# Three seven-product chunk pairs in each wide down panel, and two of their weight sums added by DMA

## The chip, the cores and the metric

The kernel runs on one core of a Trainium2 chip. The metric is the device time of one execution in microseconds, as the median of several runs. A profile of one execution comes with it: busy times, waits and DMA transfers by engine and by line of the kernel.

The engines are TensorE (PE in the profile; its weight loads are PEld), VectorE (DVE), ScalarE (ACT), GpSimd (POOL) and SyncE (SP). SP and GpSimd start DMA transfers here; a queue starts its transfers in the order in which they stand, and one that has to wait holds up those behind it.

## The reference

A decoder trunk of two layers works on 256 tokens of width 2048 in float32. The first layer mixes tokens by gated linear attention, the second by forgetting attention, and each also attends to 256 memory tokens. What the change touches is the gated MLP with hidden width 5632 that ends each layer:

```python
def conv_ffn(h, w_up, conv_w, conv_b, w_down):
    u = causal_dwconv(h @ w_up, conv_w, conv_b)
    a, val = split_cols(u, [FFN_HIDDEN, FFN_HIDDEN])
    return (jax.nn.silu(a) * val) @ w_down
```

The result of `conv_ffn` is added to the residual stream `x`.

## The kernel before

**Products in parts.** A float32 product is made of three matmuls. Each operand is split into a high part (a copy rounded to the format that TensorE multiplies, `fp32r`) and a low part (the rest). High x high, low x high and high x low are added in one PSUM bank. For weights, ScalarE makes the high part (`whi`, an ACTIVATE) and VectorE the low part (`wlo`, a subtraction) from the loaded tile `raw`. These tiles are 128 x 1024 and each of the three names has four buffers.

**The MLP.** The hidden width is 44 chunks of 128, taken in three parts of 16, 16 and 12 chunks (`PARTS`). For each part the kernel computes the up-projections, convolves and gates them (`convolve`), and keeps the activations in parts as tiles `m` (`A`, `B` or `mix` in the profile). Then it multiplies the part by `w_down`. In the first two parts of each layer, output columns 0 to 1023 are done in two ordinary panels of 512 columns, and columns 1024 to 2047 in one wide panel, `pair_tm` (line 338), which takes one chunk of 128 hidden channels after another. There are thus four such panels in the kernel, two a layer.

**A plain chunk and a seven-product pair.** For a plain chunk `pair_tm` loads 128 x 1024 weights and makes four products (two halves of the tokens by two halves of the columns), 12 matmuls (line 377), each over 512 columns. Two chunks together are a 2 x 2 block product. For the pairs that begin at a chunk in `SEVEN` (0 and 4) the kernel uses the Winograd form of Strassen's method: seven products, 21 matmuls (the helper `mm`, line 363), in place of eight products and 24. It needs four sums of activation blocks and four sums of weight blocks.

The activation sums are made in `convolve`, in temporary tiles `tsum` and then split into `asum`, one such tile for each pair. The weight sums stand in `pair_tm`: `ta` holds two of them and `tb` two (both `tsum` in the profile), 128 x 512 each, added by VectorE from the loaded weights at lines 393 to 396:

```python
V.tensor_tensor(ta[:, :512], b12, b11, ALU.subtract)
V.tensor_tensor(ta[:, 512:], b22, b12, ALU.subtract)
V.tensor_tensor(tb[:, :512], b22, ta[:, :512], ALU.subtract)
V.tensor_tensor(tb[:, 512:], b21, tb[:, :512], ALU.subtract)
```

After that `split_more` (lines 325 and 326) casts and splits `ta` and `tb` like other weights. In order, a pair's products are `p1` (with `b11`), `p2` and `p3` (with the second chunk's weights), `p5` and `p7` (with `ta`), `p6` and `p4` (with `tb`). The products `p1`, `p5`, `p6` and `p7` stay in four PSUM banks until the last pair of the panel; then one copy and seven additions (lines 406 to 409, and `add_to`, line 435) combine them and add them to `x`. The plain chunks add to other banks, which are read at the panel's end.

**Buffers.** The function `room` gives out the temporary tiles. In layer 0, `tsum` tiles share two buffers (tag `blk`), `ev` (the combination's temporary) has tiles of its own, and each pair's `asum` has one. In layer 1, `tsum` tiles share three buffers (tag `wlo` of the pool `op`), and `asum` and `ev` share three others (tag `whi`).

**Order.** The kernel is written as one long sequence, and a planner orders it at build time: it simulates a timeline and gives each engine, as it comes free, the ready instruction of the highest priority. `high_priority(offset=AHEAD)` moves loads, splits and weight sums some 300 places ahead. On the chip each engine and each DMA queue keeps that order, and waits on semaphores for its data and its buffers. All weight loads are on SP's queue, and `wp` is an array in which the host has laid out the weights in the order of use. For the chunks in `SEVEN` the host stores the two column halves of a chunk in reverse (`cols[::-1]`), so that `b12` comes first.

Of the kernel before, what the change touches and what calls it, by code (L numbers as in the profile page):

```python
# [13 lines left out]
F32 = mybir.dt.float32  # L14
# [3 lines left out]
ALU = mybir.AluOpType  # L18
PSUM = bass.MemoryType.PSUM

P = 128
# [17 lines left out]
NUNIT = 1024  # L39
AHEAD = 300  # L40
WARM = 9

SEVEN = (0, 4)

FV_PARTS = ((0, 376), (376, 764), (764, 1152), (1152, 1536))

# [9 lines left out]
def _panels():  # L56

    full = list(range(KC))  # L60
    out = []

    def fm(key, w, c0, kcs=full):
        out.append((key, w, kcs, [(c0, 256)], 4))

    def tm(key, w, c0, n, kcs=full, more=()):
        out.append((key, w, kcs, [(c0, n), *more], 2))

    tm(("mv", 0), ("mem_w_kv", 0), 512, 512)
    for l in range(2):  # L70
        tm(("mk", l), ("mem_w_kv", l), 0, 512)
    tm(("mv", 1), ("mem_w_kv", 1), 512, 512)
    tm(("gv", 0), ("gla_w_in", 0), G_V, DV, more=[(G_R, RANK)])
    tm(("mq", 0), ("gla_w_in", 0), G_MQ, 512)
    for h in range(GLA_H):
        tm(("gqk", h), ("gla_w_in", 0), G_Q + h * DK, DK, more=[(G_K + h * DK, DK)])
        if h == GLA_H - 1:
            tm(("og", 0), ("gla_w_in", 0), G_OG, 512)
        if h:
            tm(("gv", h), ("gla_w_in", 0), G_V + h * DV, DV)  # L80
    for j in range(1, 3):
        tm(("og", j), ("gla_w_in", 0), G_OG + j * 512, 512)
    late = list(range(12, 16)) + list(range(12))

    def ffn(l):
        for p, (lo, hi) in enumerate(PARTS):
            for j in range(lo, hi, 2):
                tm(("up", l, j), ("ffn_w_up", l), j * P, 2 * P, more=[(HID + j * P, 2 * P)])
            last = p == len(PARTS) - 1
            for f in range(4 if last else 2):  # L90
                tm(("down", l, p, f), ("ffn_w_down", l), f * 512, 512, list(range(lo, hi)))
            for k in range(0 if last else hi - lo):
                cols = [(1024, 512), (1536, 512)]
                out.append((("pair", l, p, k), ("ffn_w_down", l), [lo + k], cols[:: -1 if k in SEVEN else 1], 1))

    for f in range(4):
        tm(("wo", 0, f), ("gla_w_out", 0), f * 512, 512, late)
    ffn(0)
    for j in range(3):
        tm(("fk", j), ("fox_w_kv", None), F_K + j * 512, 512)  # L100
    for j, (lo, hi) in enumerate(FV_PARTS):
        more = [] if j else [(F_L, FOX_H)]
        tm(("fv", j), ("fox_w_kv", None), F_V + lo, hi - lo, more=more)
    for j in range(2):
        fm(("mq", 1, j), ("fox_w_in", 0), FOX_H * HD + j * 256)
    for j in range(6):
        fm(("fq", j), ("fox_w_in", 0), j * 256)
    for f in range(4):
        tm(("wo", 1, f), ("fox_w_out", 0), f * 512, 512, late)
    ffn(1)  # L110
    return out

# [29 lines left out]
def _trunk(ctx: ExitStack, tc: tile.TileContext, xt, xtok, memt, wp, wgu, gns, gfin, cnv, par, msk, out):  # L142
    nc = tc.nc
    where, _ = _layout()
    V, S, TE = nc.vector, nc.scalar, nc.tensor
# [192 lines left out]
    def pair_tm(units, src, sums, room, out):  # L338

        bank = {}  # L340

        def new(name, tag):
            bank[name] = pacc.tile([P, 512], F32, name="acc", tag="acc") if tag == "acc" else work(tag, 2 if tag == "s" else 1)

        for name, tag in (("p1", "acc"), ("p2", "o"), ("p3", "s"), ("p5", "acc"), ("p7", "acc"), ("p6", "acc"), ("p4", "s"),
                          ("x", "t")):
            new(name, tag)
        begun = set()
        n = len(units)
        plan = []  # L350
        k = 0
        while k < n:
            if k in SEVEN:
                plan.append(("seven", k))
                k += 2
            else:
                plan.append(("plain", k))
                k += 1
        end = [i for i, (kind, _) in enumerate(plan) if kind == "seven"][-1]

        def mm(name, x, w, last):
            for i, (a, b) in enumerate(((0, 0), (1, 0), (0, 1))):
                r = TE.matmul(bank[name], x[a], w[b], start=name not in begun, stop=last and i == 2)  # L363
                begun.add(name)
            return r

        def tok(k, b):
            return [src[k][:, part, b * P : (b + 1) * P] for part in range(2)]

        for i, (kind, k) in enumerate(plan):  # L370
            if kind == "plain":
                w = split_unit(units[k])
                last = k == n - 1
                for low in range(2):
                    for name, b, h in (("p2", 0, 0), ("p3", 0, 1), ("p4", 1, 0), ("x", 1, 1)):
                        for part in range(2 - low):
                            r = TE.matmul(bank[name], tok(k, b)[part], w[low][:, h * 512 : (h + 1) * 512],  # L377
                                          start=name not in begun, stop=last and low == 1)
                            begun.add(name)
                last_mm.append(r)  # L380
            else:
                ra, rb = load_unit(units[k]), load_unit(units[k + 1])
                b12, b11, b21, b22 = ra[:, :512], ra[:, 512:], rb[:, :512], rb[:, 512:]
                st = [[sums[k][:, part, j, :] for part in range(2)] for j in range(4)]
                done = i == end
                w = split_more(b11, 512)
                mm("p1", tok(k, 0), [t[:, :512] for t in w], done)
                w = split_more(rb, 1024)
                mm("p2", tok(k + 1, 0), [t[:, :512] for t in w], False)
                mm("p3", st[3], [t[:, 512:] for t in w], False)  # L390
                with tc.high_priority(offset=AHEAD):
                    ta, tb = room("t"), room("t")
                    V.tensor_tensor(ta[:, :512], b12, b11, ALU.subtract)
                    V.tensor_tensor(ta[:, 512:], b22, b12, ALU.subtract)
                    V.tensor_tensor(tb[:, :512], b22, ta[:, :512], ALU.subtract)
                    V.tensor_tensor(tb[:, 512:], b21, tb[:, :512], ALU.subtract)
                w = split_more(ta, 1024)
                mm("p5", st[0], [t[:, :512] for t in w], done)
                mm("p7", st[2], [t[:, 512:] for t in w], done)
                w = split_more(tb, 1024)  # L400
                mm("p6", st[1], [t[:, :512] for t in w], done)
                last_mm.append(mm("p4", tok(k + 1, 1), [t[:, 512:] for t in w], False))
                if done:
                    one, two = room("e")
                    three = room("f")
                    S.activation(one, bank["p1"], AF.Copy)
                    V.tensor_tensor(two, bank["p6"], one, ALU.add)
                    V.tensor_tensor(three, bank["p7"], two, ALU.add)
                    V.tensor_tensor(two, bank["p5"], two, ALU.add)
                    out(0, 1, two)  # L410
                    out(1, 1, three)
                    out(1, 1, bank["p5"])
                    out(1, 0, three)
                    out(0, 0, one)
        ends.append(r)
        for name, b, h in (("p2", 0, 0), ("p3", 0, 1), ("p4", 1, 0), ("x", 1, 1)):
            out(b, h, bank[name])
# [14 lines left out]

    def add_to(f):

        return lambda b, a: V.tensor_tensor(x[f][:, b, :], x[f][:, b, :], a, ALU.add)

    def turned(pool, bank, width, col, parts=False):

# [846 lines left out]
    def ffn(l, nx, h, m, ys, zs, landing, then, room, spare=None, last=None):  # L1285
        with tc.tile_pool(name=f"ffn{l}", bufs=1) as fp:
# [9 lines left out]
            sums = {}  # L1296

            def convolve(j, i, z, seven):
# [19 lines left out]
                if seven:  # L1318
                    (a11, a21), (a12, _) = [[r[:, b * P : (b + 1) * P] for b in range(2)] for r in rs]
                    a22 = rs[1][:, P:]  # L1320
                    t = room("s")[:, :512].rearrange("p (j n) -> p j n", j=4)
                    V.tensor_tensor(t[:, 0, :], a21, a22, ALU.add)
                    V.tensor_tensor(t[:, 1, :], t[:, 0, :], a11, ALU.subtract)
                    V.tensor_tensor(t[:, 2, :], a11, a21, ALU.subtract)
                    V.tensor_tensor(t[:, 3, :], a12, t[:, 1, :], ALU.subtract)
                    sums[i] = room(i)
# [19 lines left out]
            for p, (lo, hi) in enumerate(PARTS):  # L1346
# [18 lines left out]
                add_out(("down", l, p), m, hooks={(0, 2): lambda: close(1), (1, 4 if end else 3): lambda: close(0)}, **down)  # L1365
                if not end:
                    units = [where[("pair", l, p, k)][0] for k in range(hi - lo)]
                    pair_tm(units, m, sums, room, lambda b, h, a: add_to(2 + h)(b, a))

    def preparing(name, dst, pool, far, kept=None, tag="blk"):  # L1370

# [39 lines left out]
    with tc.tile_pool(name="stash", bufs=1) as st:  # L1411
# [4 lines left out]
        with tc.tile_pool(name="turn1", bufs=1) as tp:  # L1416
# [3 lines left out]
            def room(kind):  # L1420
                if kind in ("t", "s"):
                    return tp.tile([P, NUNIT], F32, name="tsum", tag="blk", bufs=2)
                if kind == "e":
                    return [tp.tile([P, 512], F32, name=f"ev{i}", tag=f"ev{i}") for i in range(2)]
                if kind == "f":
                    return tp.tile([P, 512], F32, name="ev2", tag="ev2")
                return tp.tile([P, 2, 4, P], F32R, name="asum", tag=f"asum{kind}")
# [12 lines left out]
    with tc.tile_pool(name="store", bufs=1) as op:  # L1440
# [44 lines left out]
        def room(kind):  # L1485
            if kind in ("t", "s"):
                return op.tile([P, NUNIT], F32, name="tsum", tag="wlo", bufs=3)
            if kind == "e":
                t = op.tile([P, NUNIT], F32, name="ev", tag="whi", bufs=3)
                return t[:, :512], t[:, 512:]  # L1490
            if kind == "f":
                return op.tile([P, 512], F32, name="ev2", tag="ev2")
# [74 lines left out]
```

## Time and profile before

| | |
|---|---|
| median of 3 runs | 2233.59 us (2232.02 to 2234.88) |
| the profiled execution | 2233.26 us |
| its span, first to last instruction | 2231.5 us |
| matmuls | 10405 |
| weight sums on VectorE, lines 393 to 396 | 8 each (two pairs in four panels) |
| DMA instructions of GpSimd in the profile | none listed |
| moved by DMA | 513.34 MB, mean 230 GB/s |

A line of a group or a tile names the line of the kernel, the engine, the operation, the tile written and those read (`wlo<-raw,whi`), the shape and the count (`x16`); durations are in ns as least, median and most. A line of a timeline gives start and duration in microseconds, and in brackets the time that the engine had been idle and what ended it. A line of waits gives the instruction that waited, what it waited for, the sum in microseconds, the count and the longest. A line with two times and a colon is one stretch of the execution, with each engine's busy time and its number of instructions. Matmuls overlap in the pipeline, so the time that one costs is read from start to start and not from its duration.

### The profile page before, as it was taken

To read this page: it belongs to the slowest core of one execution; us is meant where nothing else is said; L and a number is where in the kernel's file an instruction comes from. 1 tells how busy PE (TensorE), PEld (TensorE's weight loads), DVE (VectorE), ACT (ScalarE), POOL (GpSimd) and SP (SyncE) were. 2 spreads that over 40 slices of the span, in tenths; PEclk is the share of its full clock that TensorE was granted. 3 is DMA by queue.
4 is the path that set the end of the run, shared out by engine and by line. 5 is a ranking of instruction groups with operands and counts; after the bars stand their busy time and mean duration, and the time that the engine had idled before them with its cause. 6 is when DMAs were issued, how large, how long until landed. Compare 5 with 4: busy or idle time off the path is not lost.

```text
span 2231.5 us, 29658 instructions
## 1 busy us (share of the span) xinstructions
PE 2220.2 (99%) x10405; PEld 1869.1 (84%) x10405; DVE 1647.4 (74%) x2754; ACT 1200.5 (54%) x1779; POOL 3.4 (0%) x19
## 2 busy tenths in 40 slices
PE   9999999999999999999999999999999999999998
PEld 7888888888888888888888998888888888888886
DVE  7768977668777687866777569666877677775776
ACT  6655664555554455545565455454655455553554
POOL 0000000000000000000000000000000000000000
PEclk9999999999999999999999999999999999999999
DMA  9777667777776777667787767778786678766774
GB/s 348 231 222 223 194 187 244 250 234 247 246 223 205 227 241 244 204 213 237 240 244 251 214 195 244 226 244 258 242 242 201 217 237 242 242 200 217 240 245 142
DMA packets 183053, 513.34 MB, mean 230 GB/s; under 512 B 20588, under 2 KB 66296, under 8 KB 182776
## 3 DMA queue, kind: packets, MB, share of 16 engines
q1 hardware_dynamic: 182328, 510.66, 73.2%
q8 instruction: 81, 1.33, 0.2%
q10 hardware_dynamic: 576, 0.79, 0.1%
q14 instruction: 68, 0.56, 0.1%
HBM read 468.63 MB, written 42.74 MB: 229 GB/s over the span
## 4 chain that ended last, share of the span: by engine, by line
PE 98%; DMA 1%; DVE 1%; ACT 0%; SPq 0%; issue 0%; DVEq 0%
PE acc L310 71%; PE ps_s L310 9%; PE acc L282 5%; PE ps_s L377 3%; PE acc L238 3%; PE ps_o L377 1%; PE ps_t L377 1%; PE acc L236 1%; PE acc L363 1%; PE ps_s L363 0%; PE ps_s L959 0%; DMA fky<-far 0%; DMA raw<-wp 0%; PE ps_o L635 0%; PE ps_s L635 0%; PE ps_o L363 0%
## 5 line engine op out<-in xcount | busy, mean ns | idle before, releaser
L208 DVE TENSOR_TENSOR wlo<-raw,whi 128x1024 fp32r<-128x1024 f32 (+4 forms) x793 | 948.2, 1198 | 502.5 <-ACT whi L207 483.4
L207 ACT ACTIVATE whi<-raw 128x1024 fp32r<-128x1024 f32 (+4 forms) x793 | 825.1, 1042 | 781.7 <-PE acc L310 504.2
L310 PE MATMUL acc<-whi,B 128*128 128x512 f32 (+3 forms) x2672 | 647.7, 380 | 0.0
L310 PEld LDWEIGHTS acc<-whi,B 128*128 128x128 f32 x2672 | 494.4, 188 | 83.5
L310 PE MATMUL acc<-whi,mix 128*128 128x512 f32 x1488 | 369.0, 389 | 0.0
L310 PE MATMUL acc<-wlo,B 128*128 128x512 f32 (+3 forms) x1336 | 352.7, 380 | 0.0
L310 PEld LDWEIGHTS acc<-whi,mix 128*128 128x128 f32 x1488 | 279.2, 188 | 57.9
L310 PEld LDWEIGHTS acc<-wlo,B 128*128 128x128 f32 x1336 | 248.2, 188 | 42.3
L310 PE MATMUL acc<-wlo,mix 128*128 128x512 f32 x744 | 200.4, 390 | 0.0
L310 PEld LDWEIGHTS acc<-wlo,mix 128*128 128x128 f32 x744 | 139.6, 188 | 28.9
L310 PE MATMUL acc<-whi,A 128*128 128x512 f32 x592 | 150.4, 389 | 0.0
L310 PEld LDWEIGHTS acc<-whi,A 128*128 128x128 f32 x592 | 111.1, 188 | 23.1
L1310 ACT ACTIVATE cv<-u,cw 128x256 f32<-128x256 f32 x176 | 95.1, 592 | 55.6 <-DVE u L1306 54.8
L310 PE MATMUL ps_s<-whi,mix 128*128 128x512 f32 x336 | 83.8, 389 | 0.0
L310 PE MATMUL acc<-wlo,A 128*128 128x512 f32 x296 | 83.6, 389 | 0.0
L1312 DVE SCALAR_TENSOR_TENSOR cv<-u,cw,cv 128x256 f32<-128x256 f32 x176 | 77.6, 478 | 0.0
L1311 DVE SCALAR_TENSOR_TENSOR cv<-u,cw,cv 128x256 f32<-128x256 f32 x176 | 76.0, 472 | 0.0
L310 PEld LDWEIGHTS ps_s<-whi,mix 128*128 128x128 f32 x336 | 63.0, 188 | 13.0
L310 PEld LDWEIGHTS acc<-wlo,A 128*128 128x128 f32 x296 | 55.4, 188 | 11.4
L1314 ACT ACTIVATE cv<-cv 128x256 f32<-128x256 f32 x88 | 36.7, 418 | 35.3 <-DVE cv L1312 31.7
L310 PE MATMUL ps_s<-whi,B 128*128 128x512 f32 x208 | 52.5, 389 | 0.0
L238 PE MATMUL acc<-mix,whi 128*128 128x512 f32 x192 | 48.9, 394 | 0.0
(346 smaller groups left out, 2062.8 us busy)
## 6 DMA issues: line engine op xcount, KB each, us to landing
raw<-wp SPq DMA_DIRECT2D x743, 512.0 KB, 4.3
fvt<-far SPq DMA_DIRECT2D x100, 128.0 KB, 5.8
raw<-wp SPq DMA_DIRECT2D x32, 384.0 KB, 3.4
yzu<-far SPq DMA_DIRECT2D x96, 128.0 KB, 5.7
far<-yu SPq DMA_DIRECT2D x22, 512.0 KB, 2.8
far<-yzu SPq DMA_DIRECT2D x22, 512.0 KB, 2.9
raw<-wp SPq DMA_DIRECT2D x24, 388.0 KB, 3.7
far<-blk SPq DMA_DIRECT2D x12, 512.0 KB, 3.4
```

What stands on the lines that cost most here:

```text
L207: casts.append(S.activation(hi[:, s], raw[:, s], AF.Copy))
L208: lows.append(V.tensor_tensor(lo[:, s], raw[:, s], hi[:, s].bitcast(F32), ALU.subtract))
L236: mm = TE.matmul(acc[p][c][:, :T], w[:, s], both[:, 0, :], start=False, stop=end and j == 3)
L238: mm = TE.matmul(acc[p][c], w[:, s], both, start=u == j == 0, stop=end and j == 3)
L282: mm = TE.matmul(acc[b][:, :n], src[kcs[j] - base][:, part, b * P : (b + 1) * P], w, start=u == 0 and low == part == j == 0, stop=u == end ...
L310: mm = TE.matmul(acc[b][:, :n], src[kc - base][:, part, b * P : (b + 1) * P], ready[low][:, j * n : (j + 1) * n], start=i == low == part = ...
L363: r = TE.matmul(bank[name], x[a], w[b], start=name not in begun, stop=last and i == 2)
L377: r = TE.matmul(bank[name], tok(k, b)[part], w[low][:, h * 512 : (h + 1) * 512], start=name not in begun, stop=last and low == 1)
L1310: S.activation(r, u[:, 2:], AF.Identity, bias=w[3], scale=w[2])
L1311: V.scalar_tensor_tensor(r, u[:, 1 : T + 1], w[1], r, ALU.mult, ALU.add)
L1312: V.scalar_tensor_tensor(r, u[:, :T], w[0], r, ALU.mult, ALU.add)
L1314: S.activation(cv[0], cv[0], AF.Silu)
```

## The change

`SEVEN` becomes (0, 4, 8): in each wide panel a third pair, chunks 8 and 9, is done with seven products. The signs of the scheme are changed so that all weight sums are additions, and two of the four move to the DMA engines: SP loads the first chunk's weights a second time into `ta` (512 KB, `b11` and `b12`), and then two accumulating transfers issued by GpSimd add `b12` to its first half and `b22` to its second (256 KB each, from `wp` in device memory). VectorE keeps the two sums of `tb`. The activation sums and the final combination follow with changed signs. In layer 0 `ev` moves into the two `blk` buffers, in layer 1 into the three `wlo` buffers, since three `asum` tiles now fill `whi`. The host no longer reverses the column halves.

```diff
-SEVEN = (0, 4)
+SEVEN = (0, 4, 8)
...
                 ra, rb = load_unit(units[k]), load_unit(units[k + 1])
-                b12, b11, b21, b22 = ra[:, :512], ra[:, 512:], rb[:, :512], rb[:, 512:]
+                ta = room("t")
+                source = [wp[u[0] : u[0] + P * NUNIT].rearrange("(p n) -> p n", p=P) for u in units[k : k + 2]]
+                with tc.high_priority(offset=AHEAD):
+                    nc.sync.dma_start(ta, source[0])
+                    nc.gpsimd.dma_start(ta[:, :512], source[0][:, 512:], accum_op=ALU.add)
+                    nc.gpsimd.dma_start(ta[:, 512:], source[1][:, 512:], accum_op=ALU.add)
+                b11, b21, b22 = ra[:, :512], rb[:, :512], rb[:, 512:]
...
-                    ta, tb = room("t"), room("t")
-                    V.tensor_tensor(ta[:, :512], b12, b11, ALU.subtract)
-                    V.tensor_tensor(ta[:, 512:], b22, b12, ALU.subtract)
-                    V.tensor_tensor(tb[:, :512], b22, ta[:, :512], ALU.subtract)
-                    V.tensor_tensor(tb[:, 512:], b21, tb[:, :512], ALU.subtract)
+                    tb = room("t")
+                    V.tensor_tensor(tb[:, :512], b22, ta[:, :512], ALU.add)
+                    V.tensor_tensor(tb[:, 512:], b21, tb[:, :512], ALU.add)
...
                     S.activation(one, bank["p1"], AF.Copy)
-                    V.tensor_tensor(two, bank["p6"], one, ALU.add)
+                    out(0, 0, one)
+                    V.tensor_tensor(two, one, bank["p6"], ALU.subtract)
...
-                    out(0, 1, two)
-                    out(1, 1, three)
-                    out(1, 1, bank["p5"])
+                    out(0, 1, two, ALU.subtract)
+                    out(1, 1, three, ALU.subtract)
+                    out(1, 1, bank["p5"], ALU.subtract)
                     out(1, 0, three)
-                    out(0, 0, one)
...
                 if kind == "e":
-                    return [tp.tile([P, 512], F32, name=f"ev{i}", tag=f"ev{i}") for i in range(2)]
+                    t = tp.tile([P, NUNIT], F32, name="ev", tag="blk", bufs=2)
+                    return t[:, :512], t[:, 512:]
...
             if kind == "e":
-                t = op.tile([P, NUNIT], F32, name="ev", tag="whi", bufs=3)
+                t = op.tile([P, NUNIT], F32, name="ev", tag="wlo", bufs=3)
```

More of the change, by code (lines that the diff above doesn't have):

```diff
@@ L93, in ffn @@
                 cols = [(1024, 512), (1536, 512)]
-                out.append((("pair", l, p, k), ("ffn_w_down", l), [lo + k], cols[:: -1 if k in SEVEN else 1], 1))
+                out.append((("pair", l, p, k), ("ffn_w_down", l), [lo + k], cols, 1))
     for f in range(4):
@@ L433, in add_to @@
     def add_to(f):
-        return lambda b, a: V.tensor_tensor(x[f][:, b, :], x[f][:, b, :], a, ALU.add)
+        return lambda b, a, op=ALU.add: V.tensor_tensor(x[f][:, b, :], x[f][:, b, :], a, op)
     def turned(pool, bank, width, col, parts=False):
@@ L1321, in convolve @@
                     t = room("s")[:, :512].rearrange("p (j n) -> p j n", j=4)
-                    V.tensor_tensor(t[:, 0, :], a21, a22, ALU.add)
-                    V.tensor_tensor(t[:, 1, :], t[:, 0, :], a11, ALU.subtract)
+                    V.tensor_tensor(t[:, 0, :], a22, a21, ALU.subtract)
+                    V.tensor_tensor(t[:, 1, :], t[:, 0, :], a11, ALU.add)
                     V.tensor_tensor(t[:, 2, :], a11, a21, ALU.subtract)
@@ L1367, in ffn @@
                     units = [where[("pair", l, p, k)][0] for k in range(hi - lo)]
-                    pair_tm(units, m, sums, room, lambda b, h, a: add_to(2 + h)(b, a))
+                    pair_tm(units, m, sums, room, lambda b, h, a, op=ALU.add: add_to(2 + h)(b, a, op))
     def preparing(name, dst, pool, far, kept=None, tag="blk"):
```

## The prediction

> **What bounds the kernel.** I read the page's first part and its chain first, then TensorE's waits.
>
> ```profile
> span 2231.5 us, 29658 instructions
> PE 2220.2 (99%) x10405; PEld 1869.1 (84%) x10405; DVE 1647.4 (74%) x2754; ACT 1200.5 (54%) x1779; POOL 3.4 (0%) x19
> ...
> PE 98%; DMA 1%; DVE 1%; ACT 0%; SPq 0%; issue 0%; DVEq 0%
> ...
> PE ps_o L182 <- DVE B L179: 1.4, 1, 1.4
> PE ps_t L545 <- DVE dg L543: 0.8, 1, 0.8
> PE acc L282 <- ACT whi L207: 0.2, 1, 0.2
> ```
>
> TensorE is the bound: 98% of the chain, and three waits of 2.4 us in all, none of them on a line of the pair panels (L363, L377). So no engine but TensorE can give time back there, and one that comes late enough can only take it. The next views are the timeline of TensorE over the first pair panel and the panel's matmuls by line.
>
> ```profile
> 675.57 0.62 PE L363 MATMUL acc<-whi,mix 128*128 128x512 f32 x2
> ...
> 693.48 0.62 PE L377 MATMUL ps_o<-whi,mix 128*128 128x512 f32 x2
> ...
> 696.20 0.62 PE L377 MATMUL ps_o<-whi,mix 128*128 128x512 f32 x2
> ...
> 717.96 1.98 PE L310 MATMUL acc<-whi,B 128*128 128x512 f32 x8
> ...
> 675.50:718.00 42.50, 10.52 (x42) 7.75 (x42) 1.00 0.62 199
> ...
> 675.50:718.00 42.50, 33.38 (x144) 27.04 (x144) 1.00 0.62 199
> ```
>
> The last two rows are the stretch of the panel with L363 alone and with L377 alone: 42 matmuls in two pairs of 21, and 144 in twelve plain chunks of 12. One plain chunk goes from 693.48 to 696.20: 2.72 us for 12, or 0.2267 us each. The panel lasts from 675.57 to the next panel's first matmul at 717.96, 42.39 us; 186 matmuls at that pace are 42.17. The missing 0.22 us is a slightly slower pace about the two pairs, 0.11 us a pair, and no hole.
>
> **The change, part by part.** *Matmuls.* Chunks 8 and 9 take 21 matmuls in place of 24. There are four pair panels (two parts in each of two layers), which I take as alike, so 12 matmuls go: 12 x 0.2267 = 2.72 us, all on TensorE. Four more pairs at the slower pace give back 4 x 0.11 = 0.44. What is left is 2.28 us, 0.10% of the time. A change within 0.2% (4.5 us) is about what a measurement of this kernel can't tell from none.
>
> *VectorE and ScalarE.*
>
> ```profile
> L325 ACT ACTIVATE whi<-tsum x16: 1042/1062/1065, 672.6 to 1991.9; 128x1024 fp32r<-128x1024 f32 x16
> L326 DVE TENSOR_TENSOR wlo<-tsum,whi x16: 1218/1221/1226, 673.7 to 1995.0; 128x1024 fp32r<-128x1024 f32 x16
> ...
> L1322 DVE TENSOR_TENSOR tsum<-cv,cv x8: 282/286/293, 530.8 to 1863.4; 128x128 f32<-128x128 f32 x8
> ...
> L621 ACT ACTIVATE asum<-tsum x8: 615/616/617, 537.4 to 1867.4; 128x512 fp32r<-128x512 f32 x8
> L622 DVE TENSOR_TENSOR asum<-tsum,asum x8: 684/684/685, 539.1 to 1868.6; 128x512 fp32r<-128x512 f32 x8
> L393 DVE TENSOR_TENSOR tsum<-raw x8: 684/685/693, 663.5 to 1981.8; 128x512 f32<-128x512 f32 x8
> ...
> L396 DVE TENSOR_TENSOR tsum<-raw,tsum x8: 683/684/686, 667.9 to 1988.3; 128x512 f32<-128x512 f32 x8
> ...
> 660.00:700.00 40.00, 40.00 (x177) 32.97 (x176) 34.53 (x44) 20.08 (x22) 0.00 (x0) 1.00 0.62 197
> ...
> 700.00:718.00 18.00, 18.00 (x81) 14.89 (x81) 8.79 (x8) 7.12 (x7) 0.00 (x0) 1.00 0.69 207
> ```
>
> The last two rows give busy time of TensorE, its weight loads, VectorE, ScalarE and GpSimd in two stretches. Two plain chunks cost VectorE 2 x 1.22 = 2.44 us. A pair costs a 512-wide split (0.685), three 1024-wide ones (3.66) and four sums L393 to L396 (2.74), 7.09 in all; with two sums gone 5.72. A panel gets 5.72 - 2.44 = 3.28 from the third pair and loses 2 x 1.37 = 2.74 on the other two: +0.54 us. ScalarE gets 0.62 + 3 x 1.06 - 2 x 1.06 = 1.68. Both hide: VectorE is busy 34.53 of 40 us before 700 and only 8.79 of 18 after it, where most of the third pair falls. The third set of activation sums adds 4 x 0.286 + 0.684 = 1.83 us of VectorE and 0.62 of ScalarE to a part's up-projections. Without cover all of VectorE's share would be 4 x 2.37 = 9.5 us; its 74% over the span says that it has cover. The final combination moves too. It needs the last pair's products, which end after 21 + 24 + 21 + 24 + 21 = 111 matmuls, at about 675.57 + 25.2 + 0.33 = 701.1:
>
> ```profile
> 692.08 0.69 DVE L407 TENSOR_TENSOR ev<-acc,ev 128x512 f32<-128x512 f32 x1 [0.26 <-PE acc L363]
> ...
> 699.09 0.68 DVE L435 TENSOR_TENSOR x<-x,acc 128x512 f32<-128x512 f32 x1
> ```
>
> From L407 to the end of the last add that reads one of these PSUM banks is 7.7 us now, so about 709 afterwards. The next panel wants a bank at about 717.4. Cost nothing, with 8 us to spare.
>
> *The accumulating DMAs.* Here lies the risk. Sum tile `ta` is now a 512 KB load on SP's queue, then two 256 KB accumulations on GpSimd's queue that wait for it, then cast and split as before. The trace has no accumulation, so its price is bounded by the nearest rows (KB each, median us to landing; the first row is from 660 to 712 us, the second and last from the first 40 us):
>
> ```profile
> raw<-wp SPq DMA_DIRECT2D x20, 512.0 KB, 4.4
> ...
> q1 hardware_dynamic: 6190, 12.91, 89.7%
> ...
> raw<-wp SPq DMA_DIRECT2D x18, 512.0 KB, 5.6
> ...
> mt<-memt SPq DMA_DIRECT2D x7, 256.0 KB, 7.1
> ...
> out<-x SPq DMA_DIRECT2D x4, 256.0 KB, 3.3
> ```
>
> An accumulation brings 256 KB and must also read 256 KB back, so I take it as a 512 KB load of this stage, 4.4 us; ends 3.3 and 7.1. Both of one tile run together; the second I put 0.8 us behind (its 256 KB at about 330 GB/s, the 512 KB of a load over its share of the stage), ends 0 and a whole one more. GpSimd does nothing else in the panel (0.00 us), so behind a waiting accumulation stand only the next ones. One `ta` then takes 4.4 + 4.4 + 0.8 = 9.6 us from its issue on SP.
>
> When can it be issued, and when is it needed?
>
> ```profile
> 659.35 2.19 SPq L335 DMA_DIRECT2D raw<-wp  x2
> ...
> 672.64 1.06 ACT L325 ACTIVATE whi<-tsum 128x1024 fp32r<-128x1024 f32 x1 [2.11 <-PE acc L310]
> ...
> 673.74 1.23 DVE L326 TENSOR_TENSOR wlo<-tsum,whi 128x1024 fp32r<-128x1024 f32 x1
> 675.47 0.69 DVE L393 TENSOR_TENSOR tsum<-raw 128x512 f32<-128x512 f32 x1
> ...
> 676.93 1.10 PE L363 MATMUL acc<-whi,asum 128*128 128x512 f32 x4
> ...
> 687.47 1.09 PE L363 MATMUL acc<-whi,asum 128*128 128x512 f32 x4
> ...
> 1717.18 3.40 SPq L335 DMA_DIRECT2D raw<-wp  x2
> ...
> 1735.93 0.86 PE L363 MATMUL acc<-whi,asum 128*128 128x512 f32 x3
> ```
>
> First pair, layer 0: SP has issued both weight loads by 661.5; 661.5 + 9.6 = 671.1, while the cast waits for a buffer until 672.64 anyway and TensorE wants it at 676.93. Hidden, with 4.7 us to spare after the cast. Second pair: layer 0 has two buffers for `ta` and `tb`, so its `ta` waits for the first one's split, 673.74 + 1.23 = 674.97 (L393 now starts right after it, at 675.47). 674.97 + 9.6 = 684.6, cast to 685.6, and the products want it at 687.47: 1.9 us to spare. Third pair: its buffer comes free when the second's split ends, 685.6 + 1.2 = 686.8; ready 696.4, cast 697.5. Wanted 12 + 24 + 9 = 45 matmuls after 687.47, at 697.7: 0.2 us to spare, plus the nine products of chunk 10 that need no sum (2.0 us), if the planner puts them ahead. Layer 1 has three buffers: the second `ta` can follow its weight loads (1720.6 + 9.6 + 1.06 = 1731.3, wanted at 1735.93), and the third takes a buffer some 18 us before its turn. So I cost the DMAs at nothing, hidden by plain chunks; in layer 0 that is thin.
>
> *SP's queue.* Behind a `ta` that waits for its buffer stand later weight loads. They mostly wait for buffers as it is:
>
> ```profile
> SPq L202 <- DVE wlo L208: 992.1, 515, 9.4
> ```
>
> In layer 0 the third `ta` waits to about 686.8, with the loads of its own pair ahead of it, and all four raw buffers are then taken. Cost nothing unless it waits longer.
>
> *Sum.* The profiled execution took 2233.26 us (span 2231.5 and 1.76 around it), 0.33 under the median of the three runs. 2233.26 - 2.28 = 2231.0 us.
>
> **Rivals.** *The 16 DMA engines fill up.* The profile counts one set of 16 engines for all queues. From 660 to 700 they move 197 GB/s at a share of 0.62, so 3.15 us of all engines per MB. A pair adds a 0.52 MB load and two accumulations of 0.26, counted once or twice: 1.05 to 1.57 MB, 3.3 to 4.9 us; three pairs 9.9 to 14.8 us in the 47 us up to 707, on top of 29: a share of 0.83 to 0.94. At 0.897, in the first 40 us, a weight load took 5.6 us, not 4.4. The chain grows to 5.6 + 5.6 + 0.8 = 12.0. Layer 0's second `ta` loads in a lull (the row below is 671 to 680) and keeps its time; the third is ready at 686.8 + 12.0 = 698.8, cast at 699.9, 2.2 us late in each of two panels: 2231.0 + 4.4 = 2235.4. Against it: the nine products of chunk 10 could fill 2.0 us of that. [...]
>
> ```profile
> q1 hardware_dynamic: 283, 1.02, 41.8%
> ```
>
> *The accumulations are slow: the case on the slower side.* At 7.1 us each, layer 0's second `ta` is ready at 687.3, its cast ends at 688.3, 0.9 us late; the third is issued at 689.6, ready 701.9, cast 702.9, against 698.6: 4.3 more. 5.2 us in each of two panels: 2231.0 + 10.4 = 2241.4. If they also run one after the other, the chain is 18.6 us, the two are 7.2 and 10.6 us late, and the time is near 2231.0 + 35.6 = 2267. It outweighs the saving once layer 0's panels stop for 1.1 us each, and the 0.2% once they stop for 3.4. For it: the thin spare time, a queue that no row shows; against it: most 512 KB loads of the stage land in 4.4. [...]
>
> *Faster by over 0.2%.* TensorE's pace about the pairs could lose its excess, 4 x 0.22 = 0.9 us, with the sums off VectorE: 2230.1. That is still within 0.2%; only scatter or a luckier order elsewhere gives more.
>
> **How the numbers follow.** Hidden as summed (2231.0): 0.48, nearly all within 0.2%. DMA engines full (2235.4): 0.17, two thirds within 0.2% and one third slower. Slow or serial accumulations (2241 and up): 0.30, slower. Faster by over 0.2%: 0.04; the rest, 0.01, within. Together faster 0.04, within 0.2% 0.60, slower 0.36. The likeliest is 2231.0, on its own 2229 to 2234. The range for 8 in 10 goes from 2229 to 2244, which leaves out the serial end and the lucky one.
>
> **What would show it.** Right: 183 matmuls in each pair panel and some 41.8 us to the next panel (42.39 now), 732 matmuls on the two lines where 744 were; two sums a pair on VectorE, 12 of each; GpSimd's queue landing its accumulations within 4 to 5 us; TensorE waiting nowhere on L363 or L377. Wrong: TensorE waits at L363 on ScalarE's cast of `tsum`, which waits on a DMA, in layer 0's panels (rivals one and two, told apart by the DMA share there); or a panel in which raw weights come late because SP stood behind a `ta`.

## The result and the profile after

The changed kernel takes 2248.97 us (median; 2245.58 to 2250.67) where the kernel before takes 2233.49 us on the same chip: 1.0068 times as long, with a 95% interval of 1.0050 to 1.0085. It is slower by 15.5 us. The forecast was 2231.0 us, and its range ended at 2244.

The profiled execution after took 2245.58 us, the lowest of its runs, against 2233.26 us before; its span grew by 12.3 us. The other three runs took 2247.95 to 2250.67; no trace shows where they lost the rest. From the page of the kernel after, the first part, the DMA queues and the chain by engine:

```profile
span 2243.8 us, 29806 instructions
PE 2222.1 (99%) x10393; PEld 1868.2 (83%) x10393; DVE 1654.7 (74%) x2774; ACT 1206.8 (54%) x1791; POOL 24.6 (1%) x43
...
q0 software_dynamic: 3456, 6.29, 1.6%
...
PE 96%; DMA 2%; DVE 1%; ACT 0%; issue 0%; SPq 0%; POOL 0%; DVEq 0%; ACTq 0%; POOLq 0%
```

The 12 matmuls are gone (10393 for 10405). A new queue, q0, carries GpSimd's transfers, and the chain that ended last now holds 2% of DMA where it held 1%. TensorE's waits show where (instruction, what it waited for, sum, times, longest):

```profile
PE acc L363 <- ACT whi L325: 10.2, 3, 5.2
PE ps_o L182 <- DVE B L179: 1.5, 1, 1.5
PE acc L282 <- ACT whi L207: 0.7, 1, 0.7
```

The first row is new: TensorE waits at a pair's products for ScalarE's cast, three times. The timeline of TensorE gives the ends of the first panel of layer 0, with the gap inside it and the first matmuls of chunk 10 behind it (708.41), and of the first panel of layer 1:

```profile
675.46 0.62 PE L363 MATMUL acc<-whi,mix 128*128 128x512 f32 x2
...
698.49 0.40 PE L363 MATMUL ps_s<-wlo,asum 128*128 128x512 f32 x1
704.12 2.92 PE L363 MATMUL acc<-whi,asum 128*128 128x512 f32 x6 [5.23 <-ACT whi L325]
...
708.41 0.63 PE L377 MATMUL ps_o<-whi,mix 128*128 128x512 f32 x2
...
725.21 1.52 PE L310 MATMUL acc<-whi,B 128*128 128x512 f32 x6
...
1736.97 0.62 PE L363 MATMUL acc<-whi,mix 128*128 128x512 f32 x2
...
1778.83 1.52 PE L310 MATMUL acc<-whi,mix 128*128 128x512 f32 x6
```

Layer 0's first panel lasts 725.21 - 675.46 = 49.75 us (42.39 before), layer 1's first 1778.83 - 1736.97 = 41.86. The same reading gives 49.17 and 41.92 for the second panels. So layer 1 gains 0.5 us a panel as forecast, and layer 0 loses 7.4 and 6.8. That is 14.1 us lost and 1.0 gained, 13.1 in all, where the span shows 12.3. Most of the difference was won between the layers: 745.00 us pass from the end of layer 0's second panel to layer 1's first, where 746.05 passed before.

The chain of waits about the gap (start, duration, what) shows one stop:

```profile
689.23 4.23 DMA tsum<-wp
...
693.53 0.49 issue
694.02 7.53 DMA tsum<-wp
...
701.57 0.70 DVE tsum L399
...
702.30 0.70 DVE tsum L400
...
703.01 1.06 ACT whi L325
...
704.12 2.92 PE acc L363 x6
```

At 689.23 the third pair's `ta` gets its buffer (the split of the second pair's `ta` ended at 689.2) and is loaded in 4.2 us. Then GpSimd starts the accumulations at 694.02; the first has landed 7.5 us later, the second at about 702.8. After the cast, TensorE goes on at 704.12. The price that the prediction had to guess stands in the part on DMA issues (KB each, median us to landing):

```profile
tsum<-wp SPq DMA_DIRECT2D x12, 512.0 KB, 4.5
tsum<-wp POOLq DMA_DIRECT2D x24, 256.0 KB, 8.0
```

An accumulation of 256 KB lands 8.0 us after its issue, later than any of the rows that bounded it. The stop also costs more than its length. Stretches of the first panel (length, busy time and count of TensorE, weight loads, VectorE, ScalarE and GpSimd, then the granted clock, the DMA share and GB/s):

```profile
690.00:698.40 8.40, 8.40 (x38) 6.92 (x38) 4.34 (x5) 2.26 (x3) 1.75 (x2) 1.00 0.77 233
698.40:704.20 5.80, 0.57 (x4) 0.13 (x2) 1.49 (x3) 1.19 (x2) 0.00 (x0) 0.76 0.61 125
704.20:708.20 4.00, 4.00 (x10) 3.13 (x11) 4.00 (x5) 4.00 (x5) 0.00 (x0) 0.50 0.36 121
708.20:715.00 6.80, 6.80 (x31) 5.62 (x30) 6.80 (x8) 3.21 (x4) 0.00 (x0) 1.00 0.78 271
```

For 4.0 us after the stop the granted clock is 0.50: ten matmuls where the last row's pace (31 in 6.80 us) gives eighteen, so about 1.8 us more. The stop of 5.4 us, this and 0.6 us at the second pair come to 7.8 of the 7.9 us by which the panel exceeds layer 1's 41.86.

### The profile page after: what moved, and what is told of

The parts are those of the page before. It is cut to its first block, busy times and chain, and to the rows that moved or that the text cites. A ratio compares the mean times of both kernels' runs of the same rounds, so it can differ in the third digit from the quotient of the medians.

```text
span 2243.8 us, 29806 instructions
## 1 busy us (share of the span) xinstructions
PE 2222.1 (99%) x10393; PEld 1868.2 (83%) x10393; DVE 1654.7 (74%) x2774; ACT 1206.8 (54%) x1791; POOL 24.6 (1%) x43
## 3 DMA queue, kind: packets, MB, share of 16 engines
q0 software_dynamic: 3456, 6.29, 1.6%
## 4 chain that ended last, share of the span: by engine, by line
PE 96%; DMA 2%; DVE 1%; ACT 0%; issue 0%; SPq 0%; POOL 0%; DVEq 0%; ACTq 0%; POOLq 0%
PE acc L310 70%; PE ps_s L310 9%; PE acc L282 5%; PE acc L238 3%; PE ps_s L377 2%; DMA tsum<-wp 2%; PE acc L236 1%; PE acc L363 1%; PE ps_o L377 1%; PE ps_t L377 1%; PE ps_s L363 0%; PE ps_s L963 0%; DVE wlo L326 0%; ACT whi L325 0%; PE ps_o L639 0%
## 5 line engine op out<-in xcount | busy, mean ns | idle before, releaser
L208 DVE TENSOR_TENSOR wlo<-raw,whi 128x1024 fp32r<-128x1024 f32 (+4 forms) x785 | 937.2, 1197 | 469.3 <-ACT whi L207 452.1
L207 ACT ACTIVATE whi<-raw 128x1024 fp32r<-128x1024 f32 (+4 forms) x785 | 815.5, 1041 | 747.8 <-PE acc L310 501.1
L325 ACT ACTIVATE whi<-tsum 128x1024 fp32r<-128x1024 f32 x24 | 24.7, 1056 | 52.7 <-DMA tsum<-wp 19.3
```

The lines of the kernel that those rows point to most:

```text
L207: casts.append(S.activation(hi[:, s], raw[:, s], AF.Copy))
L208: lows.append(V.tensor_tensor(lo[:, s], raw[:, s], hi[:, s].bitcast(F32), ALU.subtract))
L325: casts.append(S.activation(hi[:, :n], src, AF.Copy))
```

## Experiments

Lengths of the four wide panels, from the start of a panel's first matmul to the start of the next panel's first, in the profiled execution of each run; medians and ratios from the timed runs. Each ratio is to runs of the kernel before taken beside that run, whose medians lie between 2232.91 and 2233.49.

| run | layer 0 | layer 1 | median us | ratio (95%) |
|---|---|---|---|---|
| before (its profile) | 42.39, 42.39 | 42.41, 42.41 | 2233.49 | |
| after | 49.75, 49.17 | 41.86, 41.92 | 2248.97 | 1.0068 (1.0050 to 1.0085) |
| e1_vec | 41.81, 41.81 | 41.85, 41.85 | 2231.03 | 0.9991 (0.9982 to 0.9999) |
| e2_two | 43.71, 43.76 | 43.05, 43.33 | 2236.84 | 1.0015 (1.0006 to 1.0024) |
| e3_slot | 43.59, 43.17 | 42.41, 42.03 | 2236.27 | 1.0017 (1.0008 to 1.0025) |
| e4_spread | 44.71, 44.67 | 42.68, 42.93 | 2236.83 | 1.0019 (1.0009 to 1.0029) |
| e5_load | 41.81, 41.81 | 41.86, 41.86 | 2230.68 | 0.9989 (0.9979 to 0.9998) |
| e6_copy | 46.17, 45.51 | 42.79, 41.86 | 2236.75 | 1.0017 (1.0007 to 1.0026) |
| e8_one | 43.03, 43.10 | 41.86, 41.86 | 2233.02 | 1.0003 (0.9993 to 1.0012) |
| e11_buf3 | 42.46, 43.03 | 42.01, 43.61 | 2234.48 | 1.0006 (0.9997 to 1.0015) |
| e10_room | 41.83, 41.83 | 41.86, 41.86 | 2232.52 | 0.9997 (0.9988 to 1.0006) |
| e9_four | 41.23, 41.23 | 41.30, 41.30 | 2229.98 | 0.9987 (0.9979 to 0.9996) |

### The third pair without the DMA sums

```diff
-                    nc.sync.dma_start(ta, source[0])
-                    nc.gpsimd.dma_start(ta[:, :512], source[0][:, 512:], accum_op=ALU.add)
-                    nc.gpsimd.dma_start(ta[:, 512:], source[1][:, 512:], accum_op=ALU.add)
+                    V.tensor_tensor(ta[:, :512], b11, b12, ALU.add)
+                    V.tensor_tensor(ta[:, 512:], b12, b22, ALU.add)
```

> Three pairs as in the changed kernel, with its buffers and signs, but all four weight sums of a pair added by VectorE; no accumulating DMA. Theory (layer 0's two buffers plus accumulations of 8 us stop TensorE in front of the third pair): no stop is left, all four wide panels last 41.8 to 41.9 us as layer 1's do in the changed kernel, the time is 2233.5 - 2.1 = 2231.4 us. Rival 1 (the third pair itself is too much for VectorE and ScalarE): layer 0's panels stay near 49 us, 2245 to 2250. Rival 2 (the added DMA traffic holds up the weight loads everywhere): 2231.4 as well.

2231.03 us, 18 us under the changed kernel and 0.9991 of the kernel before. All four panels last 41.81 to 41.85 us. In the list of TensorE's waits only the one at the kernel's start is left:

```profile
PE ps_o L182 <- DVE B L179: 1.4, 1, 1.4
```

So three pairs with all their sums on VectorE are hidden, and Rival 1 falls: the loss comes with the sums by DMA, not with the third pair.

### The DMA sums without the third pair

```diff
-SEVEN = (0, 4, 8)
+SEVEN = (0, 4)
```

> Only the pairs at chunks 0 and 4, as before, with the sums of ta by accumulating DMA: the DMA part of the change alone. Theory: only layer 0's second pair is a little late, 0.6 to 1.0 us a panel by the changed kernel's rows; 2233.5 + 2 = 2235.5. Rival 1 (third pair): 2233.5, nothing lost. Rival 2 (DMA traffic): 8 of the 12 tiles remain, so two thirds of the loss, about 2244.

2236.84 us, 3.6 us over the kernel before and 12 under the changed one. The theory's 2235.5 is near, Rival 2's 2244 is not. But layer 1's panels lost too (43.05 and 43.33 for 42.41), which no theory had. In the first of them VectorE stands 3.15 us at a sum of `tb` (L399), which reads `ta` and so waits for the accumulations, and TensorE then waits for the instruction behind it, L439:

```profile
1729.95 0.69 DVE L399 TENSOR_TENSOR tsum<-raw,tsum 128x512 f32<-128x512 f32 x1 [3.15 <-DMA tsum<-wp]
1730.56 0.68 DVE L439 TENSOR_TENSOR x<-x,ps_s 128x512 f32<-128x512 f32 x1
...
1731.29 0.73 PE L363 MATMUL ps_s<-whi,mix 128*128 128x512 f32 x2 [0.34 <-DVE x L439]
```

L439 stands behind that sum in VectorE's queue and empties the PSUM bank `ps_s`, which TensorE needs next.

### The third pair's buffer earlier

```diff
-                ta = room("t")
+                ta = room("t8" if k == 8 else "t")
...
+                if kind == "t8":
+                    return tp.tile([P, NUNIT], F32, name="tsum", tag="asum0")
```

> The changed kernel, but in layer 0 the third pair's ta lies in the buffer of the first pair's activation sums (same size, free once the first pair's products are done, some 7 us before the buffer that it has now). Theory: the third pair's stop goes and the second's small one stays: 2231.4 + 2 = 2233.5. Rivals 1 and 2: no change, 2245 to 2250.

2236.27 us: 12.7 of the 15.5 us are back with one buffer moved. SP now starts the third pair's load at 681.69 (the second row), 7.5 us before the 689.23 of the changed kernel. The last two rows are from the chain of waits:

```profile
674.88 0.33 SPq L386 DMA_DIRECT2D tsum<-wp  x1
...
681.69 0.33 SPq L386 DMA_DIRECT2D tsum<-wp  x1
...
681.69 8.38 DMA tsum<-wp
...
691.14 7.13 DMA tsum<-wp
```

That is the theory's mechanism shown by itself: the accumulations still take 7.9 us over the whole execution, but they start earlier. Not all of the 7.5 us arrives: the load, now beside the second pair's accumulations and the weight loads, took 8.4 us, and the second accumulation landed at 698.3 in place of 702.8. The estimate was 2.8 us too low; the panels still stand 0.2 to 1.7 us over 41.86.

### The third pair two chunks later

```diff
-SEVEN = (0, 4, 8)
+SEVEN = (0, 4, 10)
```

> The changed kernel with the third pair at chunks 10 and 11 in place of 8 and 9, so that four plain chunks (10.9 us) stand between the second and the third pair where two stood. Theory: the added 5.4 us cover all or nearly all of the third pair's stop; with the second pair's left, 2233 to 2236. Rivals 1 and 2: 2245 to 2250.

2236.83 us, just above the 2236 that was expected at most. Two more plain chunks between the pairs remove the long stop as the earlier buffer did. Layer 0's panels still stand 2.8 us over 41.86, with waits of up to 0.7 us at two pairs. Layer 1 shows the wait of the run with two pairs again, on VectorE and then on TensorE (the last row):

```profile
1732.44 0.69 DVE L399 TENSOR_TENSOR tsum<-raw,tsum 128x512 f32<-128x512 f32 x1 [3.35 <-DMA raw<-wp]
1733.05 0.68 DVE L439 TENSOR_TENSOR x<-x,ps_s 128x512 f32<-128x512 f32 x1
...
1733.79 0.73 PE L363 MATMUL ps_s<-whi,mix 128*128 128x512 f32 x2 [0.54 <-DVE x L439]
```

VectorE stands 3.35 us at L399; the profile names the load of `raw` as what came last, where it named the DMA of `ta` in that run. So the wait that moved to the DMA engines is still a wait on VectorE's queue, and it holds up work that has nothing to do with the sums.

### Only the load, no accumulation

```diff
-                    nc.gpsimd.dma_start(ta[:, :512], source[0][:, 512:], accum_op=ALU.add)
-                    nc.gpsimd.dma_start(ta[:, 512:], source[1][:, 512:], accum_op=ALU.add)
```

> The changed kernel without its two accumulations: ta is only the 512 KB load, so this leaves the sums b12 and b22 out of ta (and the output is another). Buffers, order of the pairs, SP's loads and VectorE's work are those of the changed kernel. Theory (the two accumulations make the chain too long): without them ta lands 4.5 us after its issue, layer 0's panels last 41.8 to 42 us, 2231.4 us. Rival (the extra 512 KB load, or the wait of SP's queue for ta's buffer, is what holds TensorE up): layer 0's panels stay several us over 42, above 2236.

2230.68 us, with no stop in any panel. The second load of the weights, SP's wait for its buffer and the third pair cost nothing that can be measured; the loss of 18 us comes with the two accumulations. The rival falls.

### Plain copies in place of accumulations

```diff
-                    nc.gpsimd.dma_start(ta[:, :512], source[0][:, 512:], accum_op=ALU.add)
-                    nc.gpsimd.dma_start(ta[:, 512:], source[1][:, 512:], accum_op=ALU.add)
+                    nc.gpsimd.dma_start(ta[:, :512], source[0][:, 512:])
+                    nc.gpsimd.dma_start(ta[:, 512:], source[1][:, 512:])
```

> The changed kernel with GpSimd's two transfers as plain copies over the halves of ta (this leaves the additions out, the output is another), same sizes, same queue, same waits. It parts the price of 8.0 us. Theory G (most of it is the start on GpSimd's queue, 3.4 to 3.9 us to the first packet in the changed kernel's trace): they land in 6 to 7 us, layer 0's stops shrink by 1 to 2 us each, 2240 to 2244. Theory R (the reading back for the addition is most of it): they land in 4.4 us like a load, the stops go, 2232.

2236.75 us (its profiled execution 2240.1). Over the whole execution the copies land in 6.5 us (first row), against 8.0 for accumulations and 4.3 to 4.5 for SP's loads of twice the size. The timeline, two stretches of the first panel and a step of its chain of waits follow:

```profile
tsum<-wp POOLq DMA_DIRECT2D x24, 256.0 KB, 6.5
...
700.80 1.52 PE L363 MATMUL acc<-whi,asum 128*128 128x512 f32 x5 [2.49 <-ACT whi L325]
...
700.80:701.90 1.10, 1.10 (x5) 0.82 (x6) 1.10 (x1) 1.10 (x2) 0.00 (x0) 1.00 0.54 82
701.90:705.40 3.50, 3.50 (x10) 2.78 (x10) 3.50 (x5) 3.50 (x5) 0.00 (x0) 0.52 0.38 135
...
687.09 4.33 DMA tsum<-wp
```

So the landing is as Theory G had it: without the addition the transfers land 1.5 us sooner, and they still take 2 us more than SP's loads, though two of them together carry what one such load carries. That these 2 us are the start on GpSimd's queue is not shown; the traffic beside them may have part in it. The long stop shrinks from 5.4 to 2.7 us and the time fell further than I had expected: the saving counts twice, since the second pair's copies are also done earlier and the third pair's load starts at 687.09 (last row) in place of 689.23. In the row before it the clock is halved even after this shorter stop.

### One accumulation in place of two

```diff
-                    nc.sync.dma_start(ta, source[0])
+                    nc.sync.dma_start(ta[:, :512], source[0][:, :512])
...
-                    nc.gpsimd.dma_start(ta[:, 512:], source[1][:, 512:], accum_op=ALU.add)
...
+                    V.tensor_tensor(ta[:, 512:], b12, b22, ALU.add)
```

> The changed kernel with one accumulation in place of two: SP loads b11 into the first half of ta (256 KB), GpSimd adds b12 to it, and VectorE makes the other half, b12 + b22. Theory: one accumulation lands in 5.5 to 6 us and the load in 3.3, so the chain is 9 us in place of 12.5; the second pair's stop goes and the third is some 0.5 to 1 us late in layer 0: 2232 to 2235. Were the price all fixed cost (8 us for one as for two), 2238 to 2245.

2233.02 us, level with the kernel before. In layer 0's first panel (676 to 700 us; after that the same stretch of the changed kernel, 676 to 704, and last this run's whole execution) the rows are:

```profile
tsum<-wp POOLq DMA_DIRECT2D x2, 256.0 KB, 5.0
```

```profile
tsum<-wp POOLq DMA_DIRECT2D x4, 256.0 KB, 7.6
```

```profile
tsum<-wp POOLq DMA_DIRECT2D x12, 256.0 KB, 6.9
```

One accumulation lands in 5.0 us there, and two at once in 7.6; over the whole execution it is 6.9 against 8.0. So two at once took longer than one, by 2.6 us in this panel and by 1.1 over all. The shorter chain leaves 1.2 us a panel in layer 0 and nothing in layer 1. Even one accumulation a pair thus costs about as much as the third pair gains.

### A third buffer in layer 0

```diff
-                    return tp.tile([P, NUNIT], F32, name="tsum", tag="blk", bufs=2)
+                    return tp.tile([P, NUNIT], F32, name="tsum", tag="blk", bufs=3)
...
-            us = [fp.tile([P, T + 2], F32, name=f"u{i}") for i in range(4)]
+            us = [fp.tile([P, T + 2], F32, name=f"u{i}") for i in range(2)]
...
-                        r = fp.tile([P, T], F32, name=f"cv{c}", tag=f"cv{c}", bufs=3)
+                        r = fp.tile([P, T], F32, name=f"cv{c}", tag=f"cv{c}", bufs=2)
```

> The changed kernel, accumulations and all, with a third buffer for ta and tb in layer 0, as layer 1 has. The room comes from the convolution's tiles (two u in place of four, two cv of a kind in place of three). Theory: both of layer 0's stops go, its panels come near layer 1's 41.9 us; 2231.5 to 2234. Were the two buffers not what makes the accumulations' 8 us count, 2245 to 2250.

The other tiles that lie in `blk` get the third buffer as well. 2234.48 us, 14.5 under the changed kernel though all 24 accumulations are still there at 7.8 us. No wait on ScalarE's cast in front of a pair's products is left; the largest sum is VectorE's queue again:

```profile
PE ps_s L363 <- DVE x L439: 1.6, 2, 0.9
```

Two buffers with a price of 8 us are the cause: with the price lowered or a buffer added the time comes back to about that of the kernel before. It does not reach the 2231.03 of the run without DMA sums, and layer 1's second panel, with the buffers of the changed kernel, took 43.61 here for 41.92 there; what made the difference was not tried. The smaller tiles of the convolution are no help of their own, as the control below shows.

### The control, and four pairs

```diff
-SEVEN = (0, 4, 8)
+SEVEN = (0, 4, 8, 12)
```

The control has three pairs; both have VectorE's sums and the smaller tiles of the convolution, and with four pairs layer 1's `whi` has four buffers.

> Control for the smaller tiles of the convolution: three pairs, all weight sums on VectorE (2231.0 as measured), two u and two cv of a kind. If these tiles are hidden work, 2231.0 within 1 us; if the convolution now holds up TensorE, more.

> Four pairs in each wide panel (chunks 0, 4, 8 and 12), all weight sums on VectorE, with the smaller tiles of the convolution to make room for a fourth tile of activation sums. Theory (a pair's gain is 0.57 us a panel as long as its sums are hidden): another 4 x 0.57 = 2.3 us, 2228.7. Rival (VectorE, 7.1 us a pair against TensorE's 4.9, has no more room): stops in the panels, 2231 or more.

The control took 2232.52 us and four pairs 2229.98, the fastest kernel of this study: 0.9987 of the kernel before (0.9979 to 0.9996). Its first panel in TensorE's timeline lasts 716.72 - 675.49 = 41.23 us:

```profile
675.49 0.61 PE L363 MATMUL acc<-whi,mix 128*128 128x512 f32 x2
...
716.72 1.07 PE L310 MATMUL acc<-whi,B 128*128 128x512 f32 x4
```

Each pair is worth another 0.56 to 0.60 us in layer 0's panels, from 42.39 with two to 41.83 with three and 41.23 with four, and no panel has a hole. The time is 1.3 us over the 2228.7 of the estimate. The rival falls: VectorE has room for a fourth pair's sums. The control was expected within 1 us of 2231.0; its 1.5 us over the same three pairs with larger tiles is within the two intervals (0.9988 to 1.0006 and 0.9982 to 0.9999) and says nothing sure on the tiles.

## Why the prediction was wrong

**The matmuls: right.** 2.28 us were forecast for 12 matmuls; layer 1's panels after, and all four with VectorE's sums, last 41.8 to 41.9 us as the forecast said.

**VectorE, ScalarE, the final combination, SP's queue: right that they cost nothing.** The run with the load alone has them all and no stop.

**The price of an accumulation: wrong, and this is the step that failed; with it fell the term "So I cost the DMAs at nothing, hidden by plain chunks".** "I take it as a 512 KB load of this stage, 4.4 us; ends 3.3 and 7.1" was measured as 8.0, above the upper end. All the rows that bounded it were transfers that SP had started, with data moved taken as the whole price. The copies show that a pair of GpSimd's transfers lands 2 us later than such a load even without the addition (6.5 us against 4.3 to 4.5). The second accumulation was put "0.8 us behind"; it landed about 1.3 us behind the first. The chain of 9.6 us was 4.2 + 0.6 + 8.8 = 13.6 (689.23 to about 702.8). That an accumulation also reads 256 KB back was the author's estimate, and no run shows it: q0 counts 6.29 MB for the 24 accumulations and the same 6.29 MB for the 24 plain copies. VectorE's instructions did not hold GpSimd's transfers up at the third pair: VectorE stood idle for 7.23 us of that time.

```profile
701.57 0.69 DVE L399 TENSOR_TENSOR tsum<-raw,tsum 128x512 f32<-128x512 f32 x1 [7.23 <-DMA tsum<-wp]
```

**Where it strikes: right.** The slow rival named layer 0, its two buffers, and both pairs: 0.9 us late at the second pair and 4.3 more at the third. Measured are 0.6 and 5.4 in the first panel. Its 2241.4 lacked one term: the half clock after a stop adds about 1.8 us a panel. The products of chunk 10 that might have filled 2.0 us did not run. (Chunk 10 is a plain chunk, with 12 matmuls and not the nine of the prediction.) In TensorE's own order the products with `ta` stand in front of them (704.12 and 708.41 in the timeline above). On ScalarE the casts of `ta` and `tb` stand in front of chunk 10's: its weights, the first load that SP issued from 691.50 on, landed in 4.6 us, and its cast started at 704.91, behind the one of `ta` at 703.01, for which ScalarE had stood idle 10.75 us (the last row is that load).

```profile
703.01 2.00 ACT L325 ACTIVATE whi<-tsum 128x1024 fp32r<-128x1024 f32 x2 [10.75 <-DVE tsum L400]
704.91 1.04 ACT L207 ACTIVATE whi<-raw 128x1024 fp32r<-128x1024 f32 x1
...
raw<-wp SPq DMA_DIRECT2D x1, 512.0 KB, 4.6
```

At the first pair nothing was lost, but not as summed: its `ta` was loaded from 596.83 on, some 65 us before the 661.5 of the prediction.

**The chance was wrong with it.** A margin of 0.2 us at the third pair, with a price from rows of another queue, carried 0.48. With the ends of that price, 3.3 to 7.1, most of the interval had no margin at all, so slower deserved more than 0.36. The range ended at 2244, just above the slow case's 2241.4; the measured time lies 5 us beyond it and 18 us short of the serial end's 2267.

**The DMA engines full: not the cause by itself, but not excluded from the price.** The extra load brought no stop, and from 690.00 to 698.40 the DMA share was 0.77 where the rival had 0.83 to 0.94. But in the 3.8 us from the first issue at 694.02 (the first two rows) no packet of GpSimd's queue q0 moved, while SP's queue q1 kept the engines 82.3% busy. The three weight loads that SP issued from 691 to 694 landed in 6.4 us beside the third pair's load and accumulations (third row), and in 4.3 in the run with the load alone, where neither stood beside them (last row). How much of the accumulations' 8 us is the traffic beside them was not tried apart.

```profile
q1 hardware_dynamic: 242, 0.87, 82.3%
...
tsum<-wp POOLq DMA_DIRECT2D x2, 256.0 KB, 7.9
...
raw<-wp SPq DMA_DIRECT2D x3, 512.0 KB, 6.4
...
raw<-wp SPq DMA_DIRECT2D x3, 512.0 KB, 4.3
```

## What to carry to other kernels

To take work off VectorE, which was not the bound, gained nothing here: all three pairs' sums were hidden on it (2231.03 us with them there, 2230.68 with the two of `ta` left out). A transfer of another kind than the trace holds has no bound in it (8.0 us here, where the rows of before ended at 7.1): measure its time from issue to landing first, and compare it with how long its buffer is free ahead of the use, not with the engine time it saves. When a chain of load, transfer and cast runs through a ring of two buffers, try one more buffer or more work between two uses: here they brought back 14.5 and 12.1 of the 15.5 us. Look also at what stands in the waiting engine's queue behind it.

## What the runs showed of the hardware

After some stops of TensorE the granted clock fell to 0.50. In the changed kernel's first panel it fell inside the stop of 5.4 us: the 0.76 over the 5.80 us of the second stretch is 2.8 us at 0.50, and 4.0 us at 0.50 follow it. In the run with copies it fell 1.1 us after the matmuls had resumed from the stop of 2.7 us, for 3.5 us, and in the second panel 1.0 us after a stop of 2.0 us, for 3.4 us (the first row below). A matmul cost 0.427 us from start to start then (four from 705.13 to 706.84 in the changed kernel), in place of 0.227. But a stop of 2.0 us between the wide panels of layer 0 and of layer 1, in the run with the earlier buffer, left the clock at 1.00 (the last three rows, the stop and what follows it), and so did the shorter stops in the run with one accumulation (0.9 us the longest wait in front of a pair's products, and a clock of 1.00 from 675.50 to 718.00).

```profile
964.90:968.30 3.40, 3.40 (x9) 2.73 (x9) 3.40 (x5) 3.40 (x5) 0.00 (x0) 0.50 0.36 137
...
1205.40:1207.40 2.00, 0.18 (x2) 0.03 (x1) 2.00 (x6) 2.00 (x5) 0.00 (x0) 1.00 0.06 6
1207.40:1210.00 2.60, 2.60 (x12) 2.16 (x13) 2.60 (x8) 2.32 (x4) 0.00 (x0) 1.00 0.58 197
1210.00:1213.00 3.00, 3.00 (x15) 2.46 (x14) 3.00 (x4) 1.08 (x2) 0.00 (x0) 1.00 0.49 162
```

So stops of 2.7 and 2.0 us cost the clock in the run with copies, and one of 2.0 us did not in the run with the earlier buffer. The half clock after such a stop cost 1.2 to 1.4 us, an estimate from the matmuls in those stretches: the 10 in 3.50 us and the 9 in 3.40 us would take 2.27 and 2.04 us at 0.227 each. When a stop costs the clock and when not stays open.

In the changed kernel GpSimd's first accumulation for the third pair moved nothing for 3.8 us after its issue. By the medians over whole executions, two accumulations of 256 KB at once landed in 8.0 us, one in 6.9, two plain copies in 6.5, and SP's loads of 512 KB in 4.3 to 4.5. What part of this is GpSimd's start and what part the DMA engines' other work stays open.
